# Attention heads taken two at a time, one in each half of the partitions, in a two-layer decoder trunk

## The chip, the core and the metric

The kernel runs on one core of a Trainium2 chip. The metric is the device time of one execution in microseconds (us), as the median of several runs; smaller is better. Five engines work side by side: TensorE (PE, matrix products; PEld is its weight loads), VectorE (DVE), ScalarE (ACT), GpSimd (POOL) and SyncE (SP, which here issues the transfers). TensorE writes its products into PSUM, which has eight banks of 2 KB a partition; all else lies in SBUF with 128 partitions.

## The reference, cut to what matters

The input x is (1, 512, 1024) in float32. Two residual layers and a final norm are computed. Layer 0 has 8 stick-breaking heads and 8 sparse heads with two key/value groups (four query heads to a group); for 512 tokens every block of the sparse selection is allowed, so that the selected and the window branch are both plain causal attention with keys of their own, and the compressed branch has 31 keys. Layer 1 has 16 heads with a forget gate. A head is 64 wide. Each layer ends in a gated feed-forward part.

```python
# stick-breaking head
z = einsum('bqhd,bshd->bhqs', qb, k) * scale
log_keep = where(mask, log_sigmoid(-z), 0.0)
after = cumsum(log_keep, axis=3, reverse=True) - log_keep
a = where(mask, exp(log_sigmoid(z) + after), 0.0)
o = einsum('bhqs,bshd->bqhd', a, v)
# sparse head: three softmax branches, each with a gate
o = gb[..., 0:1] * o_cmp + gb[..., 1:2] * o_slc + gb[..., 2:3] * o_win
# forgetting head
s = einsum('bqhd,bshd->bhqs', qb, k) * scale + (cq[..., :, None] - cum[..., None, :])
o = einsum('bhqs,bshd->bqhd', masked_softmax(s, causal), v)
```

## The kernel before

All weights and activations are float32. The dense products split both operands into a high part and a rest (type fp32r, one pass of TensorE each) and add three products: high by high, high by rest, rest by high. This is `unit` (128 output features by 512 tokens, 8 steps of three products), `vgroup` (values, tokens in the partitions) and `proj` (output projections). They are handed out in steps by the queue `Fill`, and each step of three products of 512 columns is called a fill step here.

Attention goes head by head. `pipeline` keeps three heads in flight: scores and exponentials of one (`S`, for query blocks 3, 2, 1, 0 of 128 tokens, with 512, 384, 256 and 128 keys), transposes of the probabilities of the one before (`T`, 10 transposes in three groups, tile `t`, line 407), and the products with the values of the one before that (`V`, tile `o`). Between these pieces it gives out fill steps: 16 a head in the stick-breaking part, 3 a head in the sparse part, 12 a head in layer 1. A sparse pair of query heads has five entries in this list, since each head has two branches and a `CmpHead` stands for the compressed branch. Every matrix product has line 114, in the helper `mm`, so that rows tell them apart by tile names: `mm` dense, `s` scores, `o` values, `t` transposes.

A head's scores take two products a query block in layer 0. The first has the query's high part and its rest in the two halves of the 128 rows against the key's high part twice (`k`), the second has the high part alone, 64 rows, against the key's rest (`k2l`). In layer 1 both products have 128 rows, since the second one carries the gate sums in the free rows (`scores_gated`). The operands are made by `split_q` and `split_k`: a cast on ACT, a difference on DVE, and four to six transfers from SBUF to SBUF for a pair of heads. The values in layer 0 are whole float32 (`whole`): one product of 64 columns a key block, each of which the trace shows as two matmul records. In layer 1 they are split, `[Vh | Vl]` in 128 columns, against a high part and a rest of the probabilities (`ph`, `pl`), and `out_head` adds the two halves.

PSUM holds three banks for `s`, two for `t`, two for `mm` and one for `o`. The list order of the calls is not the order on the engines: a scheduler places the instructions, engine by engine, when the program is built.

Of the kernel before, what the change touches and what calls it, by code (L numbers as in the profile page):

```python
# [9 lines left out]
F32 = mybir.dt.float32  # L10
# [7 lines left out]
P = 128  # L18
# [7 lines left out]
# column groups of the transposed probabilities: key block -> offset  # L26
POFF = {0: 0, 1: 512, 3: 896, 2: 1024}
EOFF = [0, 128, 384, 768]
G0 = [0, 256, 512]


class Fill:
    """Queue of dense work, given out in steps; the next item's first step (its loads) runs ahead."""
# [34 lines left out]
def pipeline(heads, fill, steps):  # L68
    """Three heads in flight: scores of one, transposes of the one before, values of the one before that."""
    p1 = p2 = None  # L70
    for n, h in enumerate(list(heads) + [None, None]):
# [32 lines left out]
def trunk(ctx, tc, A):  # L104
# [10 lines left out]

    def table(last=None):
        """the table set that serves exp, ln and all the cheap functions."""
# [33 lines left out]
    identb = cp.tile([P, P], BF, name="identb")  # L151
    trib = cp.tile([P, P], BF, name="trib")
# [3 lines left out]
    tri32 = wp.tile([P, P], F32, tag="tri32", bufs=1, name="tri32")  # L156

    def load_consts():
        for t, n in ((ones, "ones"), (ident, "ident"), (tri32, "tri"), (mk, "mk"), (conv, "conv")):
            sp.dma_start(t, A[n])  # L160
        pool.tensor_copy(identb, ident)
        pool.tensor_copy(trib, tri32)
# [15 lines left out]
    def unit(src, use):  # L178
        """128 output features x 512 tokens; use(psum) evacuates."""
# [11 lines left out]
    def vgroup(srcs, n, use, allocs=(None, None)):  # L191
        """tokens on partitions, n output features; use(tb, psum) evacuates."""
# [29 lines left out]
    def feed(c, layer):  # L222
        """the scaled chunk's two parts, and its square sum."""
# [8 lines left out]
    def inv_sqrt(r, ss, n):  # L232
        """r = (ss/D + eps)^-0.5 with one Newton step."""
# [10 lines left out]
    def finish(srcs, oh, ol):  # L244
        """the last chunk of the last projection and the final norm, by halves of the tokens."""
# [14 lines left out]
        for b in range(2):  # L260
# [6 lines left out]
            ps = pp.tile([P, SEQ], F32, tag="s", bufs=3, name="s")  # L267
# [7 lines left out]
    def norm_stats(tok):  # L275
        ps = pp.tile([P, SEQ], F32, tag="s", bufs=3, name="s")
        mm(ps, ones, ACC[0], True, True)
        inv_sqrt(rstd, ps, SEQ)
        if tok:
            ps2 = pp.tile([P, SEQ], F32, tag="s", bufs=3, name="s")  # L280
# [5 lines left out]
    # ---------------------------------------------------------------- shared attention parts  # L286
    def split_q(qp, qf, name, rows=(0, 64), hi=None):
        """per head of the pair: high part in 64 partitions from rows[head], low part in the others."""
        qh = qp.tile([P, SEQ], F32R, tag="st_h", bufs=1, name="st_h")
        ql = qp.tile([P, SEQ], F32R, tag="st_l", bufs=1, name="st_l")  # L290
        act.copy(qh, qf)
        dve.tensor_sub(ql, qf, qh.bitcast(F32))
        q = qp.tile([P, 2, SEQ], F32R, tag="q2", bufs=2, name=name)
        for hd in range(2):
            r = slice(hd * 64, hd * 64 + 64)
            for d0, s in ((rows[hd], qh), (64 - rows[hd], ql)):
                sp.dma_start(q[d0:d0 + 64, hd].bitcast(F32), s[r].bitcast(F32))
            if hi is not None:
                sp.dma_start(hi[r, hd].bitcast(F32), qh[r].bitcast(F32))
        return q  # L300

    def split_k(qp, kf, tag, bufs, lo=None):
        """[kh;kh] for each head of the pair, and the pair's low parts."""
        kh = qp.tile([P, SEQ], F32R, tag="st_h", bufs=1, name="st_h")
        if lo is None:
            kl = qp.tile([P, SEQ], F32R, tag=tag + "l", bufs=bufs, name=tag + "l")
        else:
            kl = qp.tile([P, SEQ], F32R, tag="st_l", bufs=1, name="st_l")
        act.copy(kh, kf)
        dve.tensor_sub(kl, kf, kh.bitcast(F32))  # L310
        k2 = qp.tile([P, 2, SEQ], F32R, tag=tag, bufs=bufs, name=tag)
        for hd in range(2):
            for d0 in (0, 64):
                sp.dma_start(k2[d0:d0 + 64, hd].bitcast(F32), kh[hd * 64:hd * 64 + 64].bitcast(F32))
            if lo is not None:
                r = slice(hd * 64, hd * 64 + 64)
                sp.dma_start(lo[r, hd].bitcast(F32), kl[r].bitcast(F32))
        return k2, kl if lo is None else lo

    def evac(qp, ps, scale):  # L320
        f = qp.tile([P, SEQ], F32, tag="qf", bufs=2, name="qf")
# [6 lines left out]
    def put_v(vt, h0, nh, tb, ps, c0, whole=False):  # L328
        """normalised value rows, split: [Vh | Vl] per head, or whole."""
        src = ps[:, c0:c0 + nh * 64].rearrange("p (h d) -> p h d", d=64)  # L330
        r = rtok[:, tb:tb + 1]
        if whole:
            act.activation(vt[:, h0:h0 + nh, tb], src, AF.Copy, scale=r)
            return
        act.activation(vt[:, h0:h0 + nh, tb, 0:64], src, AF.Copy, scale=r)
        dve.scalar_tensor_tensor(vt[:, h0:h0 + nh, tb, 64:128], src, r,
                                 vt[:, h0:h0 + nh, tb, 0:64].bitcast(F32),
                                 op0=ALU.mult, op1=ALU.subtract)

    def scores_gated(ps, i, q, q1, hd, k2, k1):  # L340
# [3 lines left out]
        mm(ps[:, 0:w], q[:, hd, t], k2[:, hd, 0:w], True, False)  # L344
        mm(ps[:, 0:w], q1[:, hd, t], k1[:, hd, 0:w], False, True)

    def scores(ps, i, q, hd, k2, kl, kd, more=None):
        """psum[:, 0:128(i+1)] = q_i . k, head hd of the q pair and kd of the k pair."""
        w = P * (i + 1)
        t = slice(i * P, i * P + P)  # L350
# [6 lines left out]
    class Head:  # L357
        """one softmax head: S scores and exponentials, N normalise, T transpose and split, V values, O output."""

        def __init__(self, ap, q, hd, k, kd, vt, vh, get_o, first, last, more=None, gate=None, done=None, whole=False):  # L360
# [3 lines left out]
        def start(self):  # L364
# [4 lines left out]
            self.e = self.ap.tile([P, 1280], F32, tag="e", bufs=2, name="e")  # L369
            self.nm = self.ap.tile([P, NB], F32, tag="nm", bufs=2, name="nm")  # L370
            self.dn = self.ap.tile([P, NB], F32, tag="dn", bufs=2, name="dn")

        def S(self, i):
            self.start()
            w = P * (i + 1)
            ps = pp.tile([P, SEQ], F32, tag="s", bufs=3, name="s")
            if self.more is None:
                scores(ps, i, self.q, self.hd, *self.k, self.kd)
# [678 lines left out]
```

## Time and profile before

| | us |
|---|---|
| median of 3 runs | 1343.22 (1341.11 to 1343.25) |
| span of the profiled execution | 1338.6 |
| TensorE busy in it | 1309.4 (98%) |
| VectorE busy | 766.4 (57%) |
| ScalarE busy | 603.2 (45%) |
| stick-breaking part, 66 to 178 us | 112 |
| sparse part, 178 to 340 us | 162 |
| attention of layer 1, 755 to 936 us | 181 |

The span is the time from the first to the last instruction of one execution. A matmul record has a modelled length that reaches into the next one, so the cost of a product is read as the distance between the starts of records, or from the chain of waits, which gives each piece of work the time until the next piece. The granted clock of TensorE is 1.00 in all stretches of attention, its upper level of 2.4 GHz.

### The profile page before, as it was taken

The page shows a single profiled execution, that of the slowest core. Times are in us where ns is not written, and L with a number is a line of the kernel's source. Part 1 is how long each engine was busy: PE and PEld are TensorE (multiplying, and loading weights), DVE is VectorE, ACT ScalarE, POOL GpSimd, SP SyncE. Part 2 cuts the span into 40 slices and gives each one's busy share as a digit, 9 for nine tenths or more (in the row PEclk, how much of TensorE's full clock was granted, in tenths as well). Part 3 has the DMA queues.
Part 4 walks back from the last instruction along what each step waited for, and adds up shares of the span by engine and source line. Part 5 has one row for each costly group of instructions (what it writes and reads, how often), then busy time and mean ns, then how long its engine had stood idle before and what let it go on. Part 6 is the DMA issues. An engine that isn't in the chain of part 4 may idle for free.

```text
span 1338.6 us, 17058 instructions
## 1 busy us (share of the span) xinstructions
PE 1309.4 (98%) x6261; PEld 1043.1 (78%) x6261; DVE 766.4 (57%) x1337; ACT 603.2 (45%) x1093; POOL 128.1 (10%) x188
## 2 busy tenths in 40 slices
PE   6999999999999999999999999999999999999995
PEld 5776766665788888888888799898788888888884
DVE  6657764553766643555544666667766543566534
ACT  6666654545543322333333556655543322333432
POOL 0000012322400000000011111111300000000012
PEclk9999999999999999999999999999999999999997
DMA  6424341110333233333234536432333323333232
GB/s 219 139 75 141 90 121 33 32 42 16 119 95 95 91 87 106 109 97 95 81 98 115 154 112 170 125 98 87 102 95 99 102 76 105 108 95 96 86 96 85
DMA packets 54098, 133.37 MB, mean 100 GB/s; under 512 B 8608, under 2 KB 11552, under 8 KB 54016
## 3 DMA queue, kind: packets, MB, share of 16 engines
q1 hardware_dynamic: 53872, 132.26, 33.4%
q8 instruction: 50, 0.82, 0.3%
q14 instruction: 32, 0.26, 0.1%
q10 hardware_dynamic: 144, 0.02, 0.0%
HBM read 108.60 MB, written 2.10 MB: 83 GB/s over the span
## 4 chain that ended last, share of the span: by engine, by line
PE 95%; DVE 2%; DMA 1%; ACT 1%; issue 1%; POOL 0%; DVEq 0%; SPq 0%; ACTq 0%; POOLq 0%
PE mm L114 79%; PE s L114 6%; PE o L114 6%; PE t L407 3%; DVE x L271 0%; DVE xl L230 0%; DMA wc<-wcv 0%; ACT whi L174 0%; DMA q<-st_h 0%; DMA wraw<-wu 0%; DVE wlo L175 0%; DVE rs_u L240 0%; PE t L714 0%; DVE rstd L242 0%; DVE rs_t L237 0%
## 5 line engine op out<-in xcount | busy, mean ns | idle before, releaser
L114 PE MATMUL mm<-xh,whi 128*128 128x512 f32 x960 | 384.2, 400 | 6.3 <-ACT xh L229 6.2
L174 ACT CAST whi<-wraw 128x1024 fp32r<-128x1024 f32 (+4 forms) x223 | 203.9, 915 | 387.9 <-PE mm L114 380.0
L114 PE MATMUL mm<-xh,wlo 128*128 128x512 f32 x960 | 375.6, 391 | 1.2 <-DVE wlo L175 1.2
L114 PE MATMUL mm<-xl,whi 128*128 128x512 f32 x960 | 375.6, 391 | 0.0
L175 DVE TENSOR_TENSOR wlo<-wraw,whi 128x1024 fp32r<-128x1024 f32 (+4 forms) x223 | 236.6, 1061 | 135.4 <-ACT whi L174 132.6
L114 PEld LDWEIGHTS mm<-xh,whi 128*128 128x128 f32 x960 | 181.2, 189 | 46.1 <-issue 6.4
L114 PEld LDWEIGHTS mm<-xl,whi 128*128 128x128 f32 x960 | 180.6, 188 | 38.4 <-DVE xl L230 0.4
L114 PEld LDWEIGHTS mm<-xh,wlo 128*128 128x128 f32 x960 | 181.1, 189 | 35.8 <-DVE wlo L175 1.8
L114 PE MATMUL mm<-gh,wlo 128*128 128x512 f32 (+1 forms) x363 | 139.0, 383 | 0.0
L114 PE MATMUL mm<-gl,whi 128*128 128x512 f32 (+1 forms) x363 | 139.0, 383 | 0.0
L114 PE MATMUL mm<-gh,whi 128*128 128x512 f32 (+1 forms) x363 | 139.0, 383 | 0.0
L385 ACT ACTIVATE e<-e,nm 128x512 f32<-128x512 f32 (+3 forms) x128 | 71.8, 561 | 67.4 <-DVE nm L383 66.3
L395 POOL TENSOR_SCALAR e<-e,dn 128x512 f32<-128x512 f32 (+3 forms) x128 | 71.0, 568 | 296.8 <-DVE dn L390 176.0
L383 DVE CUSTOM_DVE_ANT_0 e<-s,mk 128x512 f32<-128x512 f32 (+3 forms) x128 | 62.0, 487 | 62.5 <-PE s L114 60.6
L792 DVE TENSOR_TENSOR a<-mm,rstd 128x512 f32<-128x512 f32 x44 | 30.4, 691 | 90.6 <-PE mm L114 90.4
L114 PE MATMUL o<-ph,vt 128*64 128x512 f32 (+7 forms) x256 | 81.3, 414 | 0.0
L114 PEld LDWEIGHTS mm<-gh,whi 128*128 128x128 f32 x363 | 68.2, 188 | 13.3
L114 PEld LDWEIGHTS mm<-gh,wlo 128*128 128x128 f32 x363 | 68.2, 188 | 13.3
L114 PEld LDWEIGHTS mm<-gl,whi 128*128 128x128 f32 x363 | 68.2, 188 | 13.3
L484 DVE TENSOR_TENSOR x<-x,mm 128x512 f32<-128x512 f32 x63 | 43.2, 686 | 55.3 <-PE mm L114 55.2
L800 DVE TENSOR_TENSOR b<-mm,rstd 128x512 f32<-128x512 f32 x44 | 30.4, 692 | 71.6 <-PE mm L114 71.3
L796 ACT ACTIVATE tt<-tt 128x512 f32<-128x512 f32 x44 | 27.8, 632 | 87.2 <-DVE tt L795 87.2
(164 smaller groups left out, 1749.5 us busy)
## 6 DMA issues: line engine op xcount, KB each, us to landing
wraw<-wfi SPq DMA_DIRECT2D x88, 512.0 KB
wraw<-wu SPq DMA_DIRECT2D x32, 512.0 KB
wraw<-wfo SPq DMA_DIRECT2D x32, 384.0 KB
wraw<-wfo SPq DMA_DIRECT2D x32, 320.0 KB
wraw<-wo SPq DMA_DIRECT2D x32, 256.0 KB
k<-st_h SPq DMA_DIRECT2D x56, 128.0 KB
q<-st_h SPq DMA_DIRECT2D x48, 128.0 KB
x<-x SPq DMA_DIRECT2D x16, 256.0 KB
```

The lines of the kernel that those rows point to most:

```text
L114: pe.matmul(out, l, r, start=st, stop=sp_)
L174: act.copy(h, w)
L175: dve.tensor_sub(l, w, h.bitcast(F32))
L383: dve.tensor_tensor_reduce(ei, ps[:, 0:w], mk[:, 384 - P * i:512], scale=-1.0, scalar=3.0e38, op0=ALU.add, op1=ALU.min, accum_out=nm)
L385: act.activation(ei, ei, AF.Exp, bias=nm, scale=-1.0, accum_out=dn)
L395: pool.tensor_scalar(ei, ei, self.dn[:, i:i + 1], 1.0, op0=ALU.mult, op1=ALU.mult)
L407: pe.transpose(ps[:, o0:o0 + P], self.e[:, EOFF[i] + j * P:EOFF[i] + j * P + P], ident)
L484: dve.tensor_add(X[m], X[m], ps)
L792: dve.tensor_mul(a, ps, rstd)
L796: silu.append(act.activation(t, t, AF.Silu).ins)
L800: dve.tensor_mul(b, ps, rstd)
```

## The change

Two heads are now worked on together (`Pair`, `SbPair`), one in partitions 0 to 63 and one in 64 to 127. A query or key tile is used as it is evacuated: no high part, no rest, no copies between partitions. A score is one whole float32 product of 64 rows for each head, and the two heads' products alternate; both write their own bank of a tile of two banks. The values are whole float32 products of 64 columns everywhere, the two heads' products alternating too. The causal mask of a stick-breaking pair is added by two bfloat16 products of 64 rows a head and block; the gate sums of layer 1 by one fp32r product of 64 rows a head and block (`sel`, `ch`). The sparse heads are put in another order (`NPERM`), so that a pair has one head of each key/value group. `pipeline` takes pairs and gives out 32 fill steps a pair in the stick-breaking part, 6 in the sparse part and 24 in layer 1. The compressed branch is no entry of its own any more. PSUM holds two tiles of two banks for `s` and one bank for `t`; the probabilities go through `t` in five groups of four transposes a pair.

```diff
+def pipeline(pairs, fill, steps):
+
         if h is not None:
-            seq.append(lambda: h.S(3))
+            seq.append(lambda: (h.S((3,)), h.S((2,))))
         if p2 is not None:
-            seq.append(lambda: p2.V(0))
-        if h is not None:
-            seq.append(lambda: h.S(2))
-        if p2 is not None:
-            seq += [lambda: p2.V(1), p2.O]
+            seq.append(p2.V)
+        if p1 is not None:
+            seq.append(lambda: p1.T(0))
         if h is not None:
             seq.append(lambda: h.N(2))
         if p1 is not None:
-            seq.append(lambda: p1.T(0))
-        if h is not None:
-            seq.append(lambda: h.S(1))
-        if p1 is not None:
             seq.append(lambda: p1.T(1))
         if h is not None:
-            seq += [lambda: h.S(0), lambda: h.N(0)]
+            seq.append(lambda: h.S((0, 1)))
         if p1 is not None:
             seq.append(lambda: p1.T(2))
+        if h is not None:
+            seq.append(lambda: h.N(0))
+        if p1 is not None:
+            seq += [lambda: p1.T(3), lambda: p1.T(4)]
...
+    def s_banks():
+        return pp.tile([P, 2, SEQ], F32, tag="s", bufs=2, name="s")
+
+    def s_bank():
+        return s_banks()[:, 0]
...
-    def scores(ps, i, q, hd, k2, kl, kd, more=None):
-        """psum[:, 0:128(i+1)] = q_i . k, head hd of the q pair and kd of the k pair."""
-        w = P * (i + 1)
-        t = slice(i * P, i * P + P)
-        r0 = 64 * kd
-        mm(ps[:, 0:w], q[:, hd, t], k2[:, kd, 0:w], True, False)
-        mm(ps[:, 0:w], q[r0:r0 + 64, hd, t], kl[r0:r0 + 64, 0:w], False, more is None)
-        if more is not None:
-            more(ps, w, i)
...
+        def scores(self, ii, more):
+
+            ps = s_banks()
+            for i in ii:
+                w = P * (i + 1)
+                o = EOFF[i] - EOFF[ii[0]]
+                t = slice(i * P, i * P + P)
+                for hd, r in enumerate(HALF):
+                    mm(ps[:, hd, o:o + w], self.q[r, t], self.k[r, 0:w], True, more is None)
+                if more is not None:
+                    for hd, r in enumerate(HALF):
+                        more(ps[:, hd, o:o + w], r, i)
+            return ps
...
-            for j in grp:
+                self.ph = self.ap.tile([P, 2560], F32, tag="ph", bufs=1, name="ph")
+            ps = pp.tile([P, SEQ], F32, tag="t", bufs=1, name="t")
+            for hd, j in TGRP[n]:
                 for i in range(j, NB):
...
+        def V(self):
+            vt, o = self.vt(), self.get_o()
+                for hd, r in enumerate(HALF):
+                    p0 = POFF[hd][j]
+                    mm(o[r, j * P:SEQ], vt[:, self.vh + hd, j], self.ph[:, p0:p0 + w],
+                       self.first and j == 0, self.last and j == 2)
...
+            def more(ps, r, i):
+                for n in range(2):
+                    mm(ps[:, i * P:i * P + P], maskb[r, 0, n], maskb[r, 1, n], False, n == 1)
+            ps = self.scores(ii, more)
...
+            def gates(p):
+                def bias(ps, r, i):
+                    mm(ps, sel[r, p], ch[r, 0:P * (i + 1)], False, True)
+                return bias
...
-            pipeline(heads + nsa, fl, lambda n: 16 if n < 8 else 3)
+            pipeline(pairs, fl, lambda n: 32 if n < 4 else 6)
-            pipeline(heads, fl, lambda n: 12)
+            pipeline(pairs, fl, lambda n: 24)
```

The order on the engines at three places. First TensorE in the sparse part, at the window scores of the second pair of query heads: before, one head's scores of two query blocks (`k`, then `k2l`) and another head's values.

```order
L114 MATMUL s<-k_1574,q_1304 128x512
L114 MATMUL s<-k2l,q_1304 128x512
L114 MATMUL o<-ph,vt 64x512
L114 MATMUL o<-ph,vt 64x384
L114 MATMUL s<-k_1574,q_1304 128x384
L114 MATMUL s<-k2l,q_1304 128x384
L114 MATMUL o<-ph,vt 64x128
L114 MATMUL o<-ph,vt 64x256
```

And now at the same scores, where "x2" is one product of each head:

```order
L115 MATMUL s<-k,q 128x512
L372 MATMUL t<-ident,e 128x128 x4
L115 MATMUL s<-k,q 128x512
L115 MATMUL s<-k,q 128x384 x2
L115 MATMUL o<-ph,vt 64x512 x2
L115 MATMUL o<-ph,vt 64x384 x2
L115 MATMUL o<-ph,vt 64x128 x2
L115 MATMUL o<-ph,vt 64x256 x2
```

The scores are one product a head and block instead of two, and the values of a pair stand in one run. Here the scheduler has put four transposes between the two heads' first products. Of the 160 places where two heads' products belong side by side (scores and values of 20 pairs at four widths), 18 are parted by something like this.

TensorE in the attention of layer 1: before, one head's scores and another head's values, with the fill between left out.

```order
L114 MATMUL s<-k_6779,q_6699 128x512
L114 MATMUL s<-k_1_5815,q_1_5813 128x512
...
L114 MATMUL o<-ph,vt 128x512
L114 MATMUL o<-pl,vt 128x512
L114 MATMUL o<-ph,vt 128x384
L114 MATMUL o<-pl,vt 128x384
```

And now, with the same left out:

```order
L115 MATMUL s<-k,q 128x512 x2
L115 MATMUL s<-ch,sel 128x512 x2
L115 MATMUL s<-k,q 128x384 x2
L115 MATMUL s<-ch,sel 128x384 x2
...
L115 MATMUL o<-ph,vt 64x512 x2
L115 MATMUL o<-ph,vt 64x384 x2
L115 MATMUL o<-ph,vt 64x128 x2
L115 MATMUL o<-ph,vt 64x256 x2
```

Each head has a float32 product and a gate product of 64 rows where it had two products of 128 rows, and float32 values of 64 columns where it had two products of 128 columns.

ScalarE in the sparse part, the first pair, now:

```order
L350 ACTIVATE e,dn<-e,nm 128x256 x2
L350 ACTIVATE e,dn<-e,nm 128x128 x2
L373 COPY ph<-t 128x512
L639 ACTIVATE cs<-cs 128x256
L373 COPY ph<-t 128x512 x2
```

The copies that free the only transpose bank stand behind the exponentials of two heads, where before they stood behind those of one and there were two banks.

## Rows read from the trace of the kernel before

**Rows 1.** The page, busy time, share of the span and instructions of an engine.

```profile
PE 1309.4 (98%) x6261; PEld 1043.1 (78%) x6261; DVE 766.4 (57%) x1337; ACT 603.2 (45%) x1093; POOL 128.1 (10%) x188
```

**Rows 2.** Busy time by stretch: stick-breaking part, sparse part, attention of layer 1.

```profile
core 0: us, PE busy (x) PEld busy (x) DVE busy (x) ACT busy (x) POOL busy (x), PEclk, DMA share, GB/s
66.00:178.00 112.00, 111.75 (x631) 82.46 (x629) 76.26 (x128) 71.00 (x154) 1.58 (x3) 1.00 0.40 113
178.00:340.00 162.00, 161.93 (x693) 97.57 (x692) 82.88 (x273) 81.55 (x214) 39.36 (x67) 1.00 0.14 39
755.00:936.00 181.00, 181.00 (x1079) 159.66 (x1078) 124.48 (x295) 107.75 (x244) 33.26 (x64) 1.00 0.46 125
```

**Rows 3.** Dense products, TensorE's records in order: start, length (us).

```profile
699.67 0.39 PE L114 MATMUL mm<-gh,whi 128*128 128x512 f32 x1
699.90 0.39 PE L114 MATMUL mm<-gh,wlo 128*128 128x512 f32 x1
```

**Rows 4.** Chain of waits, sparse part, one head and one pair's end: start, us, records.

```profile
207.38 0.84 PE s L114 x8
...
228.01 1.65 PE o L114 x4
229.66 0.74 PE s L114 x2
230.41 0.79 PE o L114 x4
231.20 0.90 PE mm L114 x3
232.09 0.44 PE t L407 x4
232.53 0.43 PE s L114 x2
...
234.29 0.32 PE s L114 x2
...
235.68 0.66 PE s L114 x2
236.34 3.35 PE o L114 x8
...
245.73 0.84 PE s L114 x8
```

**Rows 5.** Chain of waits, two stick-breaking heads: start, us, records.

```profile
105.55 1.65 PE o L114 x4
...
123.35 1.65 PE o L114 x4
```

**Rows 6.** Chain of waits, one head of layer 1: start, us, records.

```profile
827.81 0.82 PE o L114 x4
...
829.34 0.35 PE s L114 x2
...
830.40 0.45 PE o L114 x4
...
834.14 0.23 PE s L114 x2
...
836.24 0.17 PE s L114 x2
...
838.81 0.46 PE s L114 x2
```

**Rows 7.** Lines of ACT by shape, 66 to 340 us: busy, mean ns.

```profile
L409 ACT COPY ph<-t 128x512 f32<-128x512 f32 x46 | 26.7, 583 | 18.3 <-PE t L407 17.9
L385 ACT ACTIVATE e<-e,nm 128x512 f32<-128x512 f32 x16 | 11.6, 724 | 10.9 <-DVE nm L383 10.2 <-DVE dn L390 0.7
L385 ACT ACTIVATE e<-e,nm 128x256 f32<-128x256 f32 x16 | 8.1, 508 | 5.0 <-DVE nm L383 5.0
```

**Rows 8.** Instructions that read tile `k2l`: weight loads of 64 rows, ns min/median/max.

```profile
L114 PEld LDWEIGHTS s<-k2l,q x96: 182/183/184, 39.2 to 324.3; 64*128 64x128 f32 x96
```

More of the change, by code (lines that the diff above doesn't have):

```diff
@@ L279, in norm_stats @@
         if tok:
[L280 removed]
+            ps2 = s_bank()
             for tb in range(NB):
@@ L283, in norm_stats, with evac @@
             inv_sqrt(rtok, ps2[:, :NB], NB)
[L287 to L321, printed above, removed]
+    def evac(qp, ps, scale, tag, bufs):
+        f = qp.tile([P, SEQ], F32, tag=tag, bufs=bufs, name=tag)
         if scale == 1.0:
@@ new lines, in scores, with S @@
+            return ps
+        def S(self, ii):
+            ps = self.scores(ii, self.bias)
+            for i in reversed(ii):
+                w = P * (i + 1)
+                o = EOFF[i] - EOFF[ii[0]]
+                for hd in range(2):
+                    ei = self.e[:, hd, EOFF[i]:EOFF[i] + w]
+                    nm, dn = self.nm[:, hd, i:i + 1], self.dn[:, hd, i:i + 1]
+                    dve.tensor_tensor_reduce(ei, ps[:, hd, o:o + w], mk[:, 384 - P * i:512], scale=-1.0, scalar=3.0e38,
+                                             op0=ALU.add, op1=ALU.min, accum_out=nm)
+                    act.activation(ei, ei, AF.Exp, bias=nm, scale=-1.0, accum_out=dn)
+            if self.extra is not None and 0 in ii:
+                self.extra.S()
@@ L408, in T @@
-            ph = self.ph[:, g0:g1]
-            act.copy(ph, ps[:, 0:g1 - g0])
-            if not self.whole:
-                dve.tensor_sub(self.pl[:, g0:g1], ps[:, 0:g1 - g0], ph.bitcast(F32))
-        def V(self, n):
-            if n == 0:
-                self.vt = self.vt()
-                self.o = self.get_o()
-            for j in ((0, 1), (3, 2))[n]:
-                w = SEQ - j * P
-                if self.whole:
-                    r = 64 * self.hd
-                    mm(self.o[r:r + 64, j * P:SEQ], self.vt[:, self.vh, j, 0:64],
-                       self.ph[:, POFF[j]:POFF[j] + w], self.first and j == 0, self.last and j == 2)
-                    continue
-                o, v = self.o[:, j * P:SEQ], self.vt[:, self.vh, j]
-                mm(o, v, self.ph[:, POFF[j]:POFF[j] + w], self.first and j == 0, False)
-                mm(o, v, self.pl[:, POFF[j]:POFF[j] + w], False, self.last and j == 2)
@@ new lines, in T @@
+            ps = pp.tile([P, SEQ], F32, tag="t", bufs=1, name="t")
+            for hd, j in TGRP[n]:
+                for i in range(j, NB):
+                    o = POFF[hd][j] - 512 * n + (i - j) * P
+                    pe.transpose(ps[:, o:o + P], self.e[:, hd, EOFF[i] + j * P:EOFF[i] + j * P + P], ident)
+            act.copy(self.ph[:, 512 * n:512 * n + 512], ps)
+            if self.extra is not None and n == 4:
+                self.extra.T()
+        def V(self):
+            vt, o = self.vt(), self.get_o()
+            for j in (0, 1, 3, 2):
+                w = SEQ - j * P
+                for hd, r in enumerate(HALF):
+                    p0 = POFF[hd][j]
+                    mm(o[r, j * P:SEQ], vt[:, self.vh + hd, j], self.ph[:, p0:p0 + w],
+                       self.first and j == 0, self.last and j == 2)
+            if self.done is not None:
+                self.done(o)
@@ L761, in layer0 @@
+            pairs += [h for p in range(4) for h in nsa_pairs(p)]
             part = lambda m: proj(m, [(A["wo0"][m][:, 0:4], 4)], OH[:4], OL[:4], ready=lambda: 3 in OF)
@@ L953, in layer1 @@
             fl.add(*[part(m) for m in range(NK)])
-            heads = [Head(ap, lambda p=p: fl.get(Q, p), hd, lambda p=p: fl.get(K, p), hd, lambda p=p: fl.get(VT, p // 2), (2 * p + hd) % 4,
-                          new_o, True, True, more=gated(p), done=head_done(p, hd))
-                     for p in range(8) for hd in range(2)]
-            pipeline(heads, fl, lambda n: 12)
+            pairs = [Pair(ap, lambda p=p: fl.get(Q, p), lambda p=p: fl.get(K, p), lambda p=p: fl.get(VT, p // 2),
+                          2 * (p % 2), new_o, True, True, bias=gates(p), done=pair_done(p)) for p in range(8)]
+            pipeline(pairs, fl, lambda n: 24)
             fl.all()
@@ L999, in _consts @@
     cmask = np.where(end[None, None, :] <= tok[:, :, None], 0.0, NEG).astype(f)
+    tri = np.where(q[None, :] < q[:, None], 0.0, NEG).astype(f)
+    mask2 = np.stack([np.eye(P, dtype=f).reshape(2, 64, P), tri.reshape(2, 64, P)]).transpose(2, 0, 1, 3)
+    mask2 = np.concatenate([mask2, mask2])
+    rows = np.zeros((P, 8), f)
+    for p in range(8):
+        rows[4 * p:4 * p + 2, p] = rows[66 + 4 * p:68 + 4 * p, p] = 1.0
     return dict(
         ident=np.eye(P, dtype=f),
-        tri=np.where(q[None, :] < q[:, None], 0.0, NEG).astype(f),
+        mask2=mask2, rows=rows,
         mk=np.concatenate([np.zeros((P, 384), f), np.where(q[None, :] <= q[:, None], 0.0, NEG).astype(f)], 1),
```

289 lines of the change are left out of this document (103 added, 186 removed).

## Prediction, made before the changed kernel had run

> **What bounds the kernel now.** I read the page's busy times first, then the stretches, then the chain of waits. TensorE is busy for 98% of the span, no other engine for more than 57% [rows 1]. The reader should look at the stretches next, because attention fills only three of them: TensorE is busy 111.75 of 112 us in the stick-breaking part, 161.93 of 162 in the sparse part and all of 181 in layer 1, while VectorE and ScalarE are busy for half to two thirds [rows 2]. So the time is TensorE's own work, and what matters of a product is how long it keeps the next one off. The chain gives that. A dense product of 512 columns costs 0.23 us, the distance of two starts [rows 3]; three of them, a fill step, cost 0.68.
>
> One head of the sparse part costs 0.66 + 0.74 + 0.43 + 0.32 = 2.15 us for scores and 1.65 + 0.79 = 2.44 for values [rows 4]. A head of layer 1 streams just as many columns in its scores and costs 0.46 + 0.35 + 0.23 + 0.17 = 1.21, and 0.82 + 0.45 = 1.27 for values [rows 6]. Two things are to be seen. First, the sparse scores pay 0.94 more for four changes between products of 128 rows and of 64 rows, so a visit to half an array costs some 0.24, and the fill step behind it another 0.22 (0.90 against 0.68) [rows 3, 4]. Second, whole float32 values cost about twice their split form: a half product of 64 columns still runs each of its columns through TensorE four times, with half of the array idle. A stick-breaking head takes 123.35 - 105.55 = 17.80 us [rows 5], of which 16 fill steps are 48 x 0.227 = 10.9, so 6.9 are attention.
>
> **The change, part by part.** All is counted for a pair of heads and against the profiled execution's 1338.6 us; the median of the runs, 1343.2, lies 4.6 above it, and I add the sum to the median.
>
> *The hinge.* Two heads' products now use opposite halves of TensorE and alternate. No row of before shows two such products side by side, so the price of the second one lies between nothing and its own price. I take nothing but a lag, because nothing that the pair shares is short in the rows: 896 columns of float32 values take 1.65 us [rows 4], that is, two records of 896 columns, 1.09 columns a ns; two heads at once would draw 2.17 a ns, and the dense products draw 512 in 0.227, or 2.26 [rows 3]. The scores draw from different partitions and write different banks. The lag is one record, since the two records of one product follow each other in the same half.
>
> *Values of a pair:* one head's 2.44, plus 0.2 of lag for the last product, less 0.24 for one visit instead of two: 2.4. *Scores:* as many float32 columns, 2.44 with two visits, and lags of 0.3 and 0.2 for the two groups: 2.9. *Return to dense work:* three visits at 0.22, 0.66.
>
> *Sparse part, 8 pairs:* before 2 x (2.15 + 2.44) and four returns of 0.22, 10.1; now 2.9 + 2.4 + 0.66 = 6.0; 8 x 4.1 = 33 gained. Transposes stay as they are. *Compressed branch, 4 pairs:* four products that take 3.35 - 1.65 = 1.70 [rows 4] become two of 0.23; its scores stay at 0.84: 5 gained.
>
> *Stick-breaking, 4 pairs:* before 13.8. Now 2.9 + 2.4 + 0.66, twenty transposes at 0.44/4 [rows 4] for 2.2, and the masks: eight small products deep in each half at 0.085, the price of one product of 128 columns [rows 6], 0.7. Together 8.9: 4 x 4.9 = 20 gained.
>
> *Layer 1, 8 pairs:* before 2 x (1.21 + 1.27) = 4.96, without any visit. Now 2.9 + 2.4 + 0.66 and the gate products, half of 1.21 if the halves overlap: 6.6. So 8 x 1.6 = 13 lost: here the split form was as cheap as overlapped float32, and the visits and gates come on top.
>
> *Sum of TensorE's work:* -33 - 5 - 20 + 13 = -45 us.
>
> *Order.* In 18 places something stands between the two heads' products. Each loses its overlap and may add a visit, 0.2 to 0.6; I take 0.4: +7. *One transpose bank instead of two:* the next four transposes must wait for ScalarE's copy, 0.58 [rows 7], which in the sparse part stands behind exponentials of two heads (0.51 to 0.72 each, [rows 7]). Between two groups of transposes there is about one fill step of 0.68 there, two or three steps in the other parts. If ScalarE is free, four transposes, the copy and the fill almost meet (0.44 + 0.58 against 0.44 + 0.68); behind four exponentials the copy comes 2.6 late once a pair. Bounds 0 and 8 x 3 = 24; I take 0.75 a pair, +6, since ScalarE is idle half of the sparse part [rows 2] and the scheduler has moved other products in between.
>
> *At nothing:* the casts, differences and SBUF copies of queries, keys and values that go, `out_head`, and the longer VectorE and ScalarE instructions of a pair. They run beside a TensorE that is busy 99.8% or more there. For a sparse pair ScalarE then has about 10 us of work (half of 81.55 us over four pairs of query heads, [rows 2]) against 14 of TensorE with fill; where that cover fails, what comes late is the transpose copy just priced. Fill steps only move: fewer are given out in the sparse part and the rest follows after it, dense.
>
> *Total:* -45 + 7 + 6 = -32, **1311 us**.
>
> In a sentence by itself: the Trainium skill, "TensorE: Matmul & The Clock Gate", section "Part 3: Packing small matmuls — row/col tiling", says that products in different row or column groups run at once, and gives 3.07 times for four row groups; no run here shows it yet. By that figure two halves would run about 1.5 times as fast (an estimate from that page), the pair's scores and values would cost 1 us more than in my sum, and the result would be near 1332, which the weight-load rival below covers.
>
> **The rivals.**
>
> *Nothing overlaps*, so that the alternation does not do what it says. Values and scores cost 4.9 each, less 0.24, gates 1.2, masks 1.4. A sparse pair then costs 10.2 against 10.1, a stick-breaking one 13.8 against 13.8, and a pair of layer 1 11.4 against 4.96: 8 x 6.4 = 51 lost, 5 gained in the compressed branch, 3 for waits: **1392**. For it: TensorE's starts in the trace are strictly in order, and nothing in the rows proves that a second product enters an idle half. Against it: half of the array is demonstrably idle and the read rate fits. The place that decides is layer 1. Between this end and mine lie 81 us, so that the kernel gets slower once less than about 60% of the overlap is had.
>
> *Only rows or only columns overlap.* Serial values add 2.5 a pair over 20 pairs, serial scores 2.0, gates and masks another 8 in all; less waiting, +40 to +48 on my sum: **1345 to 1360**, 1353 in the middle.
>
> *Overlap, but weight loads show.* A load takes 0.18 us [rows 8], and every float32 record has its own. If half of it showed on the 16 record slots of a pair's scores and values, 1.4 x 20 = 29 would be added: **1340**. Against it: the values of today run at the rate of their columns.
>
> *ScalarE's copies pace the sparse part.* The upper bound above, 18 more: **1329**.
>
> **How the numbers follow.** Forecast 0.55 (1296 to 1328, from the bounds of order and waits and a lag that is half or double); loads 0.12; copies 0.08; one kind of overlap only 0.10; none 0.15. A measurement of this kernel tells some 0.2%, 2.7 us, from no change. Faster takes the forecast, the copies and three quarters of the loads, 0.72; same 0.05 (the rest of the loads and a little of the half overlap); slower 0.23. The range 1294 to 1360 leaves out the case without overlap and some tails, together 0.2. It holds both signs; the likeliest case's own range is 1296 to 1328.
>
> **What would show it.** Right: in the chain of waits a pair's values as one piece of about 2.4 us for 16 records, and scores of 1.8 and 1.1 us; the starts of the two heads' records nearly together; the sparse part some 30 us shorter, the stick-breaking part some 20, and the attention of layer 1 some 10 to 15 longer. Wrong: values of 4.7 us for 16 records (no overlap in columns), scores of 3 us for the first two blocks (none in rows), or idle time of TensorE before transposes with ScalarE's copy as its end, more than 1 us a pair. A stretch of layer 1 that grows by 50 us decides for the first rival.

## The result, and the profile after

The changed kernel takes 1310.69 us (median of 4 runs, 1309.58 to 1311.2) where the kernel before took 1342.16 in the same rounds: a ratio of 0.9767, with a 95% interval of 0.9753 to 0.9781. The forecast was 1311. The span of the profiled execution is 1308.3 us against 1338.6.

The page's busy times of the changed kernel, to be read against [rows 1]:

```profile
PE 1273.0 (97%) x6349; PEld 1006.8 (77%) x6349; DVE 693.8 (53%) x1139; ACT 560.7 (43%) x955; POOL 122.8 (9%) x180
```

TensorE still bounds the kernel, and its busy time falls by 36.4 us, more than the span (30.3). So some 6 us came back as idle time. Where the gain lies is read from the places in the chain of waits where the long dense runs of the two feed-forward parts begin (start, length in us, records). First before, then after:

```profile
367.71 353.20 PE mm L114 x1557
...
973.44 348.89 PE mm L114 x1569
```

```profile
327.90 352.28 PE mm L115 x1553
...
943.13 348.88 PE mm L115 x1569
```

Layer 0 up to its feed-forward part is 39.8 us shorter. From there to the second feed-forward part it was 605.7 us and is 615.2, so layer 1 is 9.5 longer. The rest is unchanged.

The chain of waits of the changed kernel, with a stick-breaking pair, a sparse pair and a pair of layer 1, answers to [rows 4 to 6]:

```profile
66.81 1.98 PE s L115 x16
...
80.05 1.13 PE s L115 x16
...
167.21 1.70 PE s L115 x8
168.92 2.31 PE o L115 x16
...
177.57 1.06 PE s L115 x4
...
749.35 2.11 PE s L115 x12
...
753.05 2.30 PE o L115 x16
...
763.35 1.08 PE s L115 x12
```

The reader is to see that the values of a whole pair are one piece of 2.30 us with 16 records, where one head alone had 1.65 + 0.79 in the sparse part [rows 4]. The scores of a pair are two pieces, 1.70 + 1.06 in the sparse part and 2.11 + 1.08 in layer 1, where the gate products are inside.

Two of the waits of TensorE in the changed kernel (what waited, the engine and tile that ended it, us in total, times, longest):

```profile
PE t L372 <- ACT ph L373: 1.9, 3, 0.7
PE mm L115 <- DVE lt L404: 1.8, 1, 1.8
```

Longer ones stand only at the start of layer 0 and ahead of the final norm. These two lie between 122 and 142 us, at the end of the stick-breaking part. The busy times by stretch (PE, PEld, DVE, ACT, POOL, then granted clock) show what that place is like, first before, then after:

```profile
131.00:150.00 19.00, 18.75 (x134) 13.65 (x133) 16.40 (x29) 13.36 (x28) 0.53 (x1) 1.00 0.42 120
```

```profile
131.00:150.00 19.00, 15.28 (x96) 11.57 (x93) 12.48 (x21) 7.49 (x12) 0.52 (x1) 0.82 0.43 129
```

TensorE idles 3.7 us of 19 there, and its granted clock is 0.82. The records show that as a stretch at the lower level (timeline of TensorE in the changed kernel: start, length, product):

```profile
141.91 0.63 PE L115 MATMUL mm<-xh,wlo 128*128 128x512 f32 x1
142.33 0.63 PE L115 MATMUL mm<-xl,whi 128*128 128x512 f32 x1
...
147.45 0.40 PE L115 MATMUL mm<-xl,whi 128*128 128x512 f32 x1
147.69 0.40 PE L115 MATMUL mm<-xh,whi 128*128 128x512 f32 x1
```

The starts are 0.43 us apart up to 147.45 and 0.23 to 0.24 behind it. Nothing of the kind stands in the attention of before [rows 2].

The start of layer 0 has a second such stretch. TensorE waits there once, for 4.9 us, where before it waited 1.2, 2.8 and 0.8 us with work between. Before, then after:

```profile
24.30:31.20 6.90, 5.15 (x42) 5.18 (x43) 5.69 (x12) 2.81 (x5) 0.00 (x0) 1.00 0.55 156
```

```profile
24.30:31.20 6.90, 4.09 (x18) 4.12 (x19) 6.10 (x12) 2.32 (x4) 0.00 (x0) 0.52 0.57 186
```

The same 144 dense products stand ahead of the layer's first score in both kernels. They take 28.0 us instead of 26.1 (the distances from each start to the next, less the waits), and the first score starts at 40.84 us instead of 38.89.

### The profile page after: what moved, and what is told of

The parts are those of the page before. It is cut to its first block, busy times and chain, and to the rows that moved or that the text cites. A ratio compares the mean times of both kernels' runs of the same rounds, so it can differ in the third digit from the quotient of the medians.

```text
span 1308.3 us, 16468 instructions
## 1 busy us (share of the span) xinstructions
PE 1273.0 (97%) x6349; PEld 1006.8 (77%) x6349; DVE 693.8 (53%) x1139; ACT 560.7 (43%) x955; POOL 122.8 (9%) x180
## 4 chain that ended last, share of the span: by engine, by line
PE 91%; DVE 5%; ACT 1%; DMA 1%; issue 1%; SPq 0%; DVEq 0%; ACTq 0%
PE mm L115 79%; PE s L115 5%; PE o L115 4%; PE t L372 3%; DVE e L409 1%; DMA wraw<-wu 1%; DVE lt L404 1%; DVE wlo L181 1%; DVE x L277 0%; DVE acc L226 0%; DVE e L410 0%; ACT lt L401 0%; ACT whi L180 0%; DVE vlo L181 0%; DMA t<-k 0%
## 5 line engine op out<-in xcount | busy, mean ns | idle before, releaser
L373 ACT COPY ph<-t 128x512 f32<-128x512 f32 x100 | 58.2, 582 | 66.4 <-PE t L372 65.8
L348 DVE CUSTOM_DVE_ANT_0 e<-s,mk 128x512 f32<-128x512 f32 (+3 forms) x128 | 55.2, 487 | 34.9 <-PE s L115 32.5
L372 PEld LDWEIGHTS t<-ident,e 128*128 128x128 f32 x400 | 46.0, 141 | 25.4 <-ACT ph L373 10.4
```

The source lines that it names most:

```text
L348: dve.tensor_tensor_reduce(ei, ps[:, hd, o:o + w], mk[:, 384 - P * i:512], scale=-1.0, scalar=3.0e38, op0=ALU.add, op1=ALU.min, accum_out=nm)
L372: pe.transpose(ps[:, o:o + P], self.e[:, hd, EOFF[i] + j * P:EOFF[i] + j * P + P], ident)
L373: act.copy(self.ph[:, 512 * n:512 * n + 512], ps)
```

## The experiments

The theory was that two heads in opposite halves of TensorE run at once, both for scores (half of the rows) and for values (half of the columns), and that everything else is small. The rivals were that only one kind overlaps, or none, and that the gain comes from work left out elsewhere.

**Values in turn.** One head's four products, then the other's.

```diff
-            for j in (0, 1, 3, 2):
-                w = SEQ - j * P
-                for hd, r in enumerate(HALF):
+            for hd, r in enumerate(HALF):
+                for j in (0, 1, 3, 2):
+                    w = SEQ - j * P
```

> The changed kernel, but a pair's values are ordered by head: all four products of one head, then all four of the other. Same halves, same count, same mode changes; only the alternation is gone. If overlap is what pays, a pair's values go from 2.30 us to 4.5 to 4.7, 20 pairs lose 44 to 48, part of it hidden where TensorE waited anyway: 1350 to 1358 us. If the gain came from fewer changes of mode and not from overlap, nothing moves: 1310 to 1315.

Measured: 1335.21 us (1334.52 to 1336.03), ratio to before 0.9953 (0.9938 to 0.9968). That is 24.5 more than the changed kernel, so the overlap of the values is real; but it lies between the two expectations. The chain of waits of this run:

```profile
169.92 3.86 PE o L115 x15
```

A pair's values take 3.86 us and not the 4.5 or more of two heads one behind the other, though the program has them in turn. The single records show why: the second head's first one starts together with the first of the last four of the first head. A later run (long product last) tests this.

**Scores in the same half.** The scores, masks and gates of both heads use rows 0 to 63; the second head's scores are then those of the first.

```diff
-                for hd, r in enumerate(HALF):
+                for hd, r in enumerate((HALF[0], HALF[0])):
...
-                    for hd, r in enumerate(HALF):
+                    for hd, r in enumerate((HALF[0], HALF[0])):
```

> The changed kernel, but the second head's scores, masks and gate sums are computed from the first head's rows, so both heads' score products use the same half of TensorE and its output is not the reference's. If overlap in rows pays, the scores of a sparse pair go from 2.75 us to about 4.9, of a stick-breaking pair from 3.1 to 5.6, of a layer 1 pair from 3.2 to 5.8: +17, +10 and +21, 1350 to 1360 us. If rows did not overlap, 1310 to 1315.

Measured: 1352.34 us (1351.79 to 1353.55), ratio 1.0082 (1.0067 to 1.0097): as the theory said, and 0.8% slower than before. The chain of waits of this run:

```profile
774.65 4.01 PE s L115 x12
...
780.23 2.30 PE o L115 x16
...
790.52 1.96 PE s L115 x12
```

The same twelve records take 4.01 and 1.96 us instead of 2.11 and 1.08, while the values stay at 2.30. The overlap in the rows is worth 2.8 us a pair of layer 1. (The rows of TensorE and the partitions that the scores' operands are read from change together here, so this run does not tell the two apart.)

**No overlap at all.** Both edits together.

> Both edits at once: values in turn, and the second head's scores from the first head's rows (its output is not the reference's). If rows and columns overlap independently, the two losses add up, +85 to +95, and the kernel is slower than the one before: 1393 to 1403 us, near the 1392 of the rival without overlap. If one hides the other, clearly less, 1355 to 1380.

Measured: 1377.54 us (1375.86 to 1379.01), ratio 1.0268 (1.0253 to 1.0283). The chain of waits shows both prices in one kernel:

```profile
874.27 4.01 PE s L115 x12
879.85 3.86 PE o L115 x15
```

The time lies in the range that was expected if one loss hid the other, 1355 to 1380, and not in the theory's, 1393 to 1403. But that range was set before values in turn were known to cost 3.86 us a pair and not 4.5 or more, and the 3.86 stands here too. The two edits add up: 24.5 and 41.7 over the changed kernel make 66.2, and 66.9 was measured. So neither hides behind the other, and the alternation is worth 67 us, twice the gain of the whole change.

**Layer 1 as before.** Layer 0 as changed, with its order on TensorE the same, and layer 1 by the code of before, with PSUM banks for each stage.

```diff
+def pipeline1(heads, fill, steps):
+    """Three heads in flight: scores of one, transposes of the one before, values of the one before that."""
...
+    def stage(es, name, two):
+        SP["p"] = es.enter_context(tc.tile_pool(name=name, bufs=2, space=PSUM))
+        SP["two"] = two
...
+            pipeline1(heads, fl, lambda n: 12)
```

> Layer 0 of the changed kernel, layer 1 of the kernel before (split products, one head at a time, its own PSUM banks). TensorE's order in layer 0 stays the same. If layer 1 loses by the change what the chain shows (10.4 us between 680 and 943 us against 720.9 and 973.4), this runs at 1299 to 1302 us. If the longer layer 1 is only work that was moved there out of layer 0, 1309 to 1312.

Measured: 1302.11 us (1300.89 to 1303.55), ratio 0.971 (0.9693 to 0.9726), 8.6 below the changed kernel. The two marks of its chain of waits:

```profile
327.78 353.20 PE mm L150 x1557
...
933.43 348.88 PE mm L150 x1569
```

From the one to the other 605.65 us pass, as before (605.73), and layer 0 is that of the changed kernel. So layer 1 loses by the change, as forecast, and the loss is in that stretch alone.

**VectorE relieved.** Two pieces of its work go to GpSimd, most of them at the end of the stick-breaking part.

```diff
-                dve.tensor_mul(u, s, rs)
+                pool.tensor_mul(u, s, rs)
...
-                            dve.tensor_add(gt[:, half * 8:half * 8 + 8, g], v, b)
+                            pool.tensor_add(gt[:, half * 8:half * 8 + 8, g], v, b)
```

> The changed kernel with two pieces of work moved from VectorE to GpSimd: the compressed gates' small additions and one multiplication of the rotary embedding. TensorE's products are the same. Theory: VectorE, 35.65 of 41 us busy between 100 and 141 us of the changed kernel's trace, is what makes TensorE idle there for some 4 us and what stands behind the 7 us at half clock that follow (products of 512 columns 0.43 us apart instead of 0.23, some 3.4 us). Then both go: 1303 to 1307 us. Rival: the single transpose bank and the copies on ScalarE are the cause, VectorE only happens to be busy; then 1309 to 1313.

Measured: 1304.94 us (1302.62 to 1307.83), ratio 0.9721 (0.9708 to 0.9735). The time is the expected one, but the trace isn't. Of TensorE's waits in this run:

```profile
PE mm L115 <- DMA wc<-wcv: 4.4, 1, 4.4
```

The waits for VectorE are gone from that place, and one of 4.4 us for the weights of the compressed values stands there instead. The time fell, but not by what the expectation named.

**Layer 1 as before, and VectorE relieved.** Both edits.

> Layer 0 as the changed kernel has it, layer 1 as the kernel before has it, and the two pieces of VectorE's work on GpSimd. Layer 1 as before gave 1302.1 us. If the relief is worth 4 to 8 us and lies in layer 0 alone, as the theory says: 1294 to 1298. Rival, that the relief is worth nothing: 1301 to 1303.

Measured: 1296.81 us (1295.28 to 1299.29), ratio 0.9666 (0.9651 to 0.968). This is the fastest of all kernels here, some 14 below the changed one and 44 below the one before (1341.14 in the same rounds).

**Scores and values joined.** A pair's values stand directly behind the long scores of the next pair.

```diff
-            seq.append(lambda: (h.S((3,)), h.S((2,))))
-        if p2 is not None:
+            seq.append(lambda: (h.S((3,)), h.S((2,)), p2 and p2.V()))
+        elif p2 is not None:
             seq.append(p2.V)
```

> The changed kernel with a pair's values written directly behind the scores of the next pair's two long blocks, with no fill step between, so that a pair has two returns from half products to dense ones instead of three; all the products are the same. Theory: a return costs 0.22 us of TensorE's time wherever it stands, so 20 pairs give back 4.4 us: 1305 to 1308. Rival: the change from half the rows to half the columns costs as much as one to the whole array, so nothing is won: 1309 to 1313.

Measured: 1304.37 us (1303.74 to 1307.99), ratio 0.9726 (0.9711 to 0.9741), just under the theory's range. A later run takes this up.

**Values in turn, the first head's long product last.** The edit of values in turn, and another order of the first head's products.

```diff
+                for j in ((0, 3, 2, 1), (0, 1, 3, 2))[hd]:
```

> As the run with values in turn (one head's four products, then the other's), but the first head's products come in the order 512, 128, 256, 384 columns instead of 512, 384, 128, 256, so that its last four records have 1280 columns instead of 768. Theory: records of the second head's half start as soon as that half is free and at most four records of the other half are ahead of them; then 1280 columns of each pair overlap, 0.43 us more than the 0.64 of the run before, over 20 pairs 8.6 us: 1325 to 1329, with a pair's values at 3.4 us. Rival: the second head can start only a fixed time ahead, some 0.65 us, whatever stands there: 1333 to 1337 and 3.86 us.

Measured: 1326.72 us (1323.44 to 1328.47), ratio 0.9884 (0.9867 to 0.99), 8.5 below values in turn; 8.6 was expected. That the totals agree so well is partly luck: the two runs were on different chips, and in the profiled executions the granted clock between 131 and 150 us was 0.82 with values in turn and 1.00 here. The reading rests on the pieces, 3.43 us for a pair's values instead of 3.86. The chain of waits of this run, and then its products by shape in the 0.27 us from 758.33 on (count; busy us, mean ns):

```profile
783.30 3.43 PE o L115 x15
```

```profile
L115 PE MATMUL o<-ph,vt 128*64 128x512 f32 x1 | 0.6, 643 | 0.0
L115 PE MATMUL o<-ph,vt 128*64 128x256 f32 x2 | 0.6, 379 | 0.0
```

The starts of one pair's records there, with the columns of each, are:

```
first head    757.21 512  757.69 512  758.12 128  758.23 128  758.335 256  758.55 256  758.77 384  759.09 384
second head                                                   758.341 512  758.82 512  759.25 384  ...
```

The second head's first record starts 6 ns behind the first of the other's last four, and ahead of three that stand before it in the program; in the built program too, all of the second head's products stand behind the first head's, so this is not the scheduler's doing. In both runs the second head starts beside the first head's fourth record from the end, and with longer records at the end more overlaps. So a number of records counts, and not a fixed time. This settles why values in turn cost less than expected.

**The changed kernel, VectorE relieved and the joined order, side by side.** The latter two had been timed on another chip than the changed kernel, so they were run beside it, without further edits.

> The changed kernel itself, on the same chip and in the same rounds as the next three, so that effects of 2 to 6 us can be read against it and not against a run on another chip. Both theories expect the time as first measured, 1308 to 1313 us.

Measured: 1310.72 us (1307.46 to 1311.5), ratio 0.9764 (0.9751 to 0.9778): as on the other chip, 1310.69. But not every wait is the same. Where TensorE waited 1.8 us for VectorE (`lt`) above, at the products of the compressed values, this execution of the same program has:

```profile
PE mm L115 <- DMA wc<-wcv: 1.4, 1, 1.4
```

So VectorE and the weights' transfer come almost together there, and relieving VectorE alone need not take that wait away.

> The relief of VectorE again, beside the changed kernel. Its first trace did not show what the theory said: TensorE's waits for VectorE between 130 and 142 us are gone, but one wait of 4.4 us for the weights of the compressed values stands in their place, and 6 us at half clock remain, now mostly inside that wait. Theory now: the idle time is not less, but the half clock falls on waiting instead of on dense products, worth about the 3 to 4 us by which the feed-forward part of layer 0 starts earlier: 3 to 5 us below the changed kernel of these rounds. Rival: the difference to the first run was that of two chips, 0 to 1.5 us.

Measured: 1305.88 us (1304.51 to 1308.05), ratio 0.9735 (0.9722 to 0.9748), 4.8 below the changed kernel. The size is as expected, the mechanism isn't. The chains of waits, first of the changed kernel in these rounds, then of the relieved one:

```profile
168.10 2.30 PE o L115 x16
...
229.12 2.30 PE o L115 x11
...
327.08 352.32 PE mm L115 x1554
```

```profile
166.66 2.31 PE o L115 x16
...
227.18 2.31 PE o L115 x16
...
322.88 352.74 PE mm L115 x1555
```

Only 1.4 of the 4.2 us had been won when the first sparse values start, where the wait and the half clock lie behind. Nor did the half clock move into the wait: from 131 to 150 us TensorE idles 3.6 us, as in the changed kernel of these rounds, at a clock of 0.82 against 0.91.

```profile
131.00:150.00 19.00, 15.41 (x104) 13.55 (x101) 13.23 (x17) 8.05 (x13) 3.62 (x5) 0.82 0.39 120
```

The other 2.8 were won in the sparse part. The edit reaches into it (three of the six multiplications moved to GpSimd run there, at 177.80, 221.03 and 253.25 us), and the scheduler placed TensorE's products otherwise: the pair at 227.18 has its values in one run of 16 records, where in the changed kernel two of them stood apart, 2.7 us ahead of the piece at 229.12. What share each of these has in the 2.8 stays open.

> Scores and values joined again, beside the changed kernel. The first run fell to the time that the theory asked for, 1304.4 us, but on another chip than the changed kernel, and its trace speaks for the rival: from a score to a value directly 0.56 us pass, as many as from a score to a dense product, and the stretch of layer 1 is as long as before the edit. Theory (a return saved is 0.22 us saved): 4 to 5 us below the changed kernel of these rounds. Rival (the change of direction costs as much as a return): within 2 us of it.

Measured: 1304.43 us (1303.73 to 1306.75), ratio 0.9726 (0.9712 to 0.9739), 6.3 below the changed kernel, more than the theory asked for. What a visit costs is to be seen in the timeline of TensorE in the changed kernel of these rounds:

```profile
753.13 0.40 PE L115 MATMUL mm<-xl,whi 128*128 128x512 f32 x1
753.46 2.37 PE L115 MATMUL o<-ph,vt 128*64 128x512 f32 x16
755.76 0.50 PE L115 MATMUL mm<-xh,whi 128*128 128x512 f32 x1
756.10 0.40 PE L115 MATMUL mm<-xh,wlo 128*128 128x512 f32 x1
```

The last dense product ahead of the values keeps TensorE for 0.33 us instead of 0.23, and the first one behind them for 0.34: 0.21 in all. In the joined kernel's chain both are gone at that place:

```profile
745.42 2.11 PE s L115 x12
747.53 2.31 PE o L115 x16
749.83 1.59 PE mm L115 x6
```

The rival had looked only at the start behind a score, which is 0.56 us later whatever follows. It overlooked that the second dense product of a return is late too. A pair of layer 1 takes 24.85 us here against 25.07 (means of four pairs), one visit less. But that is not the whole of it. By the traces layer 0 is 3.1 us shorter and the stretch of layer 1 2.6. In layer 1 values follow scores directly in six places, which gives 1.4. The rest of its 2.6 lies ahead of layer 1's first pair: in the 11 us behind the feed-forward part the granted clock was 0.88 in the changed kernel of these rounds and 1.00 in the joined one. That is not the edit's doing, since it was 1.00 in the changed kernel's first trace and 0.88 in the joined kernel's first one, whose layer 1 therefore seemed to have won nothing. In layer 0 the scheduler made only two such places more than before, 5 against 3. So the price of a visit is confirmed in the eight places that got one less, some 1.8 us, and the greater part of the 6.3 comes from the clock, another order and other waits, which weren't taken apart.

**Relieved, and the weights earlier.** The weights of the compressed values get a buffer that is free sooner.

```diff
-                    wc = spare(1, [P, 16, 64], "wc")
+                    wc = spare(1 if key == "k" else 0, [P, 16, 64], "wc")
```

> The relief of VectorE with the weights of the compressed values in a buffer that is free earlier, so that their transfer is issued far ahead of their use; nothing else differs. Theory: the 4.4 us for which TensorE waited there are then shortened to the 2 to 2.5 us until GpSimd has the products' other operand ready, and the clock has less idle time to fall upon: 2 to 4 us below the relief alone. Rival: another wait of the same length takes its place, since VectorE, GpSimd and the queue all work in a row there: within 1.5 us of the relief alone.

Measured: 1303.66 us (1303.12 to 1304.35), ratio 0.9717 (0.9704 to 0.973), 2.2 below the relief alone; the intervals of the two ratios overlap, but the traces agree. Its stretch, its one wait there, and its marks in the chain:

```profile
131.00:150.00 19.00, 17.65 (x136) 14.30 (x136) 12.99 (x17) 9.15 (x15) 3.98 (x6) 1.00 0.45 135
```

```profile
PE mm L115 <- POOL gt L565: 1.4, 1, 1.4
```

```profile
164.01 2.31 PE o L115 x16
...
320.19 352.50 PE mm L115 x1555
```

TensorE now idles 1.35 of the 19 us, the granted clock is 1.00, the first sparse values start 2.65 earlier than with the relief alone, and the feed-forward part 2.69. Here the gain lies where the theory put it.

## Why the prediction was right, step by step

*The hinge* held. The alternation is worth 67 us (no overlap at all), in rows and in columns apart, and the forecast's first rival, 1392, is what stands on its other side: 1377.5 was measured with 0.64 us a pair still overlapping at the turn of the heads, and 20 x 0.64 = 13 more make 1390. "Only rows or only columns", 1345 to 1360, came out at 1352.3 where the rows alone were taken away, and at 1335.2 for the columns, short by the same 13.

*The lag* was wrong, with little weight. I had let the second head start a whole record late. In the trace both heads' first records start within 0.1 us; by shape, in the 0.1 us from 753.0 and from 749.3 on in the changed kernel:

```profile
L115 PE MATMUL o<-ph,vt 128*64 128x512 f32 x2 | 0.7, 643 | 0.0
...
L115 PE MATMUL s<-k,q 64*128 64x512 f32 x2 | 0.7, 693 | 0.0
```

Two records of 643 ns fill 0.7 us together; their starts are 7 ns apart. So the sum was too high by that lag: values 2.30 against 2.4, sparse scores 1.70 + 1.06 = 2.76 against 2.9, stick-breaking scores with masks 1.98 + 1.13 = 3.11 against 3.6, and scores with gates in layer 1 2.11 + 1.08 = 3.19 against 3.5.

*The estimate from the Trainium skill.* By a figure of the Trainium skill, "TensorE: Matmul & The Clock Gate", section "Part 3: Packing small matmuls — row/col tiling", I had estimated that two halves run 1.5 times as fast, for 1332 us. The measurement decides: 4.01 against 2.11 us and 1.96 against 1.08 are ratios of 1.90 and 1.81, with the visit counted in. So the 3.07 for four row groups is no measure for two halves of this kernel.

*Layer 1*: 13 forecast, 9.5 measured. With the measured 3.19 for scores and gates and 2.30 for values in each of 8 pairs the sum gives 9.5. Mechanism and place were right, and layer 1 as before confirms it with 8.6.

*Layer 0*: 45 forecast (58 less 13 for order and waits), 39.8 measured. With the measured pieces the products alone would have given 8 x (10.1 - 5.7) + 4 x (13.8 - 8.3) + 5 = 62. So 22 were lost instead of 13, and four losses have a size. The layer's first score starts 1.9 later than before, because the dense products ahead of it take 1.9 longer in the stretch at half clock shown above. From there on TensorE's waits come to 6.3 us, where they were 1.1: 5.2 more, 3.5 of them between 131 and 150 us. The clock of 0.82 costs some 3 there (0.18 x 19 = 3.4, less what falls on waits). And the records themselves give what the parted places cost. None is missing in this part, and the distances from each start to the next, less the waits, come to 33.1 us for the values, where 12 pairs at 2.30 would take 27.6, and to 39.5 for the scores with masks, where the measured pieces would take 4 x 3.11 + 8 x 2.76 = 34.5: together 10.5. The four make some 20.6 of the 22. I had priced two of them, and named neither the late start nor the clock.

*Order and the one transpose bank*: their sum was right, their shares weren't. TensorE waits 1.9 us for ScalarE's copies, not 6, and not in the sparse part but at the end of the stick-breaking part (they are among the 5.2 above). The parted places, 16 of the 18 in layer 0, cost 10.5, some 0.65 each, and not 7 at 0.4 each. That 10.5 + 1.9 = 12.4 stand against 13 is luck.

*At nothing* was wrong in one place. I had written that the longer VectorE instructions of a pair run beside a TensorE that is always busy. Where the stick-breaking part ends and the sparse keys are made, they don't: the relief together with the earlier weights takes most of that idle time and the half clock there away. The error was the use of an average over 112 us [rows 2] for a place of 20.

*Weight loads* and *ScalarE's copies* as rivals: the values of two heads take less than those of one took, so no load shows in them, and 1.9 us of waits aren't 18.

So the time came out within 1 us partly because errors of both signs met: products cheaper by 4 us in layer 0 and 3 to 4 in layer 1 than priced, and idle time, clock and order together dearer by 9.

## What to carry to other kernels

Products that need only half of the rows or columns are worth pairing in opposite halves and alternating: the second one then costs next to nothing, but each visit costs 0.2 us, so a pair's products should stand in as few runs as possible. Where a split form already fills the array, as in layer 1 here, pairing only adds the visits; measure layers apart, and keep the old form where it was full. When TensorE gets faster in a stretch, look at the other engines' busy times of that stretch and not of the kernel, since idle time there can also cost the clock.

## What the runs showed of the hardware

Each half of the array's columns takes its records in order, but not the two halves together. With one head's products behind the other's, the second head's first record started beside the first of the other's last four (758.341 and 758.335 us) and ahead of records at 758.55, 758.77 and 759.09 that stand before it in the program, as written and as built. The Trainium skill, "TensorE: Matmul & The Clock Gate", section "Part 3: Packing small matmuls — row/col tiling", has matmuls starting and ending strictly in the order of the program; these starts differ from that, and the measurement decides.

The granted clock fell to its lower level at the end of the stick-breaking part in the changed kernel, after TensorE had idled for parts of some 10 us. In two executions of the same program the stretch from 131 to 150 us had 3.7 and 3.6 us of idle time and a clock of 0.82 and 0.91, the second by this row of the changed kernel in the last rounds:

```profile
131.00:150.00 19.00, 15.37 (x105) 11.72 (x102) 13.67 (x22) 8.70 (x13) 0.53 (x1) 0.91 0.43 129
```

So the same program pays differently for the same idle time. Nor does less idle time always cost less: in the same stretch values in turn idled 2.0 us, and the run with the long product last 2.6.

```profile
131.00:150.00 19.00, 16.96 (x98) 11.86 (x97) 13.32 (x22) 8.46 (x12) 0.53 (x1) 0.82 0.41 130
```

```profile
131.00:150.00 19.00, 16.42 (x121) 13.02 (x118) 13.96 (x21) 8.12 (x14) 0.53 (x1) 1.00 0.38 126
```

The first had a clock of 0.82, the second of 1.00. In the run with 1.35 us of idle time there was no fall either. At the start of layer 0 the waits of 4.8 us in three pieces, before, had no fall behind them, and the one of 4.9 us, after, had one. What decides in general no run here shows.
